# The first adaLN vector: scale and shift chunks side by side in one tile, accumulated by one operation of 512 columns

## The chip, the cores and the metric

The kernel runs on one core of one Trainium2 chip. The metric is the time of one execution on the device, in microseconds (us). A core has a matrix engine (TensorE, PE in the rows, with PEld for the loading of its weights), a vector engine (VectorE, DVE), a scalar engine (ScalarE, ACT), a general engine (GpSimd, POOL) and a sync engine (SyncE, SP, with SPq for its queue of transfers). Each engine executes its own instructions strictly in the order in which they stand; engines wait for each other by semaphores. SBUF is the on-chip memory of 128 partitions, PSUM the small memory into which TensorE writes its sums.

## What is computed

The kernel computes a decoder block: two kinds of attention side by side, then an MLP. Only its first step matters here. A condition vector `c` is multiplied by a wide matrix; the first 2048 of the resulting 6144 numbers are a shift and a scale for the normalised input `x`, and their result `h` feeds all projections.

```python
ada = (c @ w_ada + b_ada)[:, None, :]
shift1, scale1, gate1, shift2, scale2, gate2 = jnp.split(ada, 6, axis=-1)
h = rmsnorm(x, g_norm1) * (1.0 + scale1) + shift1
proj = h @ w_in
```

Here `c` has 1024 entries, `w_ada` is 1024 x 6144, `x` and `h` are 1024 x 1024 and `w_in` is 1024 x 5452, all in float32.

## The kernel before

The matrix products are done in three passes per block, with each operand split into a rounded high part and a low rest (`h_hi`, `h_lo`, `whi`, `wlo`; helper `mm3`), so every multiplication by `h` needs both parts.

The 1024 columns of `h` are worked on as eight chunks of 128, chunk 0 to 7. For a chunk, TensorE transposes two groups of four tiles of `x` into PSUM (tile `xT`, L265); ScalarE scales and shifts each group (`hf`, L272) and rounds it (`h_hi`, L273); GpSimd subtracts to get `h_lo` (L275). For the second groups of the last two chunks VectorE does all three (L268, L269, L275). The scale and shift of a chunk are columns of the small tile `ab`.

The scale and shift are made in five passes (list `KBS`, L229): pass 0 is chunk 0, pass 1 chunk 1, pass 2 chunks 2 and 3, pass 3 chunks 4 and 5, pass 4 chunks 6 and 7. For each pass `load_ada` (L206) fetches two blocks of `w_ada`, one for the scale (j = 1) and one for the shift (j = 0), into two of four buffers `wa`. In passes 0 and 1 the scale's sum over the 1024 rows is done by TensorE (L244). All the rest is done by VectorE: 8 operations in a row, each multiplying 128 or 256 columns of `wa` by an entry of `c` per partition and adding them to `acc` (L250 the first, L252 the other seven). The column sums of `acc` over the partitions are then taken by narrow TensorE products with a vector of ones (L179, shown in the rows as L75, `pv<-onesf,acc`), into the one PSUM bank `pv`, and VectorE adds the bias and writes `ab` (L180; for the scale also L183 and L184). Since there is only one bank `pv`, the column sums of one block can only start once L180 has read those of the block before.

As soon as chunks of `h` are there, TensorE multiplies them with the first weights: those of the indexer's key (in bank `S`, with `whi`), of its first two query heads (in bank `g`, with `whi`), and of its other two (with `qi_w`; first half of the sequence in bank `S`, second in bank `tr`). ScalarE and VectorE then unpack them (L360 to L372 into `KAi`, `QAi`, `QBi`, `misc`), and the index scores, the top-k search, attention and projections follow.

The order of the instructions on each engine isn't the order of the source: a list scheduler of the framework sets it from its own estimate of durations when the program is built, so a change of one operation can move many others. Block `with tc.high_priority()` (L235) puts this stage first.

Of the kernel before, what the change touches and what calls it, by code (L numbers as in the profile page):

```python
# [9 lines left out]
F32 = mybir.dt.float32  # L10
# [7 lines left out]
ALU = mybir.AluOpType  # L18
# [3 lines left out]
P = 128  # L22
D = 1024
S = 1024
KT = D // P
# [32 lines left out]
def block_kernel(ctx: ExitStack, tc: tile.TileContext, x, c, w_ada, b_ada, g_norm1, w_in, b_forget,  # L58
                 rel_bias, w_bf, w_bd, w_out, g_norm2, w_mlp1, w_mlp2, g_final, onehot, out):
    nc = tc.nc  # L60
# [3 lines left out]
    def pool(stack, name, bufs=1, **kw):  # L64
        if kw.get("space") != DRAM:
            kw.setdefault("reuse_waits", "tile")
        return stack.enter_context(tc.tile_pool(name=name, bufs=bufs, **kw))
# [6 lines left out]
    def mm(o, l, r, start, stop):  # L74
        nc.tensor.matmul(o, l, r, start=start, stop=stop)  # L75
# [15 lines left out]
    cT = vecT[:, 0:8]  # L91

    ab = cst.tile([P, 4, KT], F32, name="ab")
# [41 lines left out]
    def newton_rstd(pl, ss, n, tag, bufs=1):  # L135
        ms = pl.tile([P, n], F32, name="ms" + tag, tag="ms" + tag, bufs=bufs)
        nc.vector.tensor_scalar(ms, ss, 1.0 / D, EPS, op0=ALU.mult, op1=ALU.add)
        r = pl.tile([P, n], F32, name="rs" + tag, tag="rs" + tag, bufs=bufs)
        nc.scalar.activation(r, ms, AF.Sqrt)
        nc.vector.reciprocal(r, r)  # L140
        t = pl.tile([P, n], F32, name="nt" + tag, tag="nt" + tag, bufs=bufs)
        nc.vector.tensor_tensor(t, r, r, op=ALU.mult)
        nc.vector.tensor_tensor(t, t, ms, op=ALU.mult)
        nc.vector.tensor_scalar(t, t, -0.5, 1.5, op0=ALU.mult, op1=ALU.add)
        nc.vector.tensor_tensor(r, r, t, op=ALU.mult)
        return r
# [5 lines left out]
    ppv = pool(ps_stack, "ppv", 1, space=PSUM)  # L152
# [24 lines left out]
    def ada_cols(acc, j, k0, n, dst, ps, rows=P):  # L177
        for k in range(n):
            mm(ps[:, k:k + 1], acc[0:rows, k * P:(k + 1) * P], onesf[0:rows, 0:1], True, True)  # L179
        nc.vector.tensor_tensor(dst[:, k0:k0 + n], ps[:, 0:n], vecT[:, 24 + j * 8 + k0:24 + j * 8 + k0 + n], op=ALU.add)  # L180

    def norm_scale(dst, g0, n):
        nc.vector.tensor_scalar(dst, dst, 1.0, None, op0=ALU.add)  # L183
        nc.vector.tensor_tensor(dst, dst, vecT[:, g0:g0 + n], op=ALU.mult)  # L184
# [10 lines left out]
    wav = w_ada.rearrange("(k p) n -> p k n", p=P)  # L195
    with ExitStack() as st1:
        p1 = pool(st1, "p1")
        sqj = p1.tile([P, D], BF16, name="sqj")
        xn = [p1.tile([P, D], F32, name=f"xn{t}") for t in range(NTT)]
        ss = p1.tile([P, NTT], F32, name="ss")  # L200
        nc.scalar.activation(ss[:, 0:1], onesf[:, 0:1], AF.Sqrt)
        def load_x(ts_):
            for t in ts_:
                nc.sync.dma_start(xn[t], xr[t * P:(t + 1) * P, :])

        def load_ada(kt0, n):  # L206
            was = []
            for j in (1, 0):
                wt = p1.tile([P, KT, 256], F32, name="wa", tag="wa", bufs=4)[:, :, 0:n * P]
                nc.sync.dma_start(wt, wav[:, :, j * D + kt0 * P:j * D + (kt0 + n) * P])  # L210
                was.append((j, wt))
            return was

        def norm_x(g):
            for t in range(4 * g, 4 * g + 4):
                nc.scalar.activation(sqj, xn[t], AF.Square, accum_out=ss[:, t:t + 1])
            r = newton_rstd(p1, ss[:, 4 * g:4 * g + 4], 4, f"a{g}")
            for t in range(4 * g, 4 * g + 4):
                nc.vector.tensor_scalar(xn[t], xn[t], r[:, t - 4 * g:t - 4 * g + 1], None, op0=ALU.mult)

        load_x(range(4))
        nc.sync.dma_start(vecs[0:8, :], c.rearrange("o (k p) -> (o k) p", p=P))
        nc.sync.dma_start(vecs[8:16, :], g_norm1.rearrange("(k p) -> k p", p=P))
        nc.sync.dma_start(vecs[16:24, :], g_norm2.rearrange("(k p) -> k p", p=P))
        nc.sync.dma_start(vecs[24:72, :], b_ada.rearrange("(k p) -> k p", p=P))
        vps = ptr.tile([P, 512], F32, name="vps", tag="tr")
        nc.tensor.transpose(vps[:, 0:P], vecs, ident)
        nc.vector.tensor_copy(vecT, vps[:, 0:P])
        KBS = ((0, 1), (1, 1), (2, 2), (4, 2), (6, 2))  # L229
        was = load_ada(*KBS[0])  # L230
        load_x(range(4, 8))
        norm_x(0)
        nc.sync.dma_start(bfg[64:64 + NH, :], b_forget.rearrange("(h o) -> h o", o=1))
        first = [misc_weights(), split_w([(0, P, win[:, :, C_QI:C_QI + P])], nc.gpsimd)]
        with tc.high_priority():  # L235
            for kb, (kt0, n) in enumerate(KBS):
                if kb:
                    was = load_ada(kt0, n)
                for j, wt in was:
                    acc = p1.tile([P, 256], F32, name="acc", tag=f"acc{j}")[:, 0:n * P]  # L240
                    if j == 1 and kb < 2:
                        ps = ppv.tile([P, 512], F32, name="pv", tag="pv")
                        for k in range(KT):
                            mm(ps[0:1, 0:n * P], cT[:, k:k + 1], wt[:, k, :], k == 0, k == KT - 1)  # L244
                        nc.vector.tensor_copy(acc[0:1, :], ps[0:1, 0:n * P])
                        ada_cols(acc, j, kt0, n, ab[:, 1 - j, :], ppv.tile([P, 512], F32, name="pv", tag="pv"), 1)
                    else:
                        for k in range(KT):
                            if k == 0:
                                nc.vector.tensor_scalar(acc, wt[:, k, :], cT[:, 0:1], None, op0=ALU.mult)  # L250
                            else:
                                nc.vector.scalar_tensor_tensor(acc, wt[:, k, :], cT[:, k:k + 1], acc, op0=ALU.mult, op1=ALU.add)  # L252
                        ada_cols(acc, j, kt0, n, ab[:, 1 - j, :], ppv.tile([P, 512], F32, name="pv", tag="pv"))
                if kb == 0:
                    norm_x(1)
                if kb == len(KBS) - 1:
                    first.append(split_w([(0, P, win[:, :, C_QI + P:C_QI + 2 * P])], nc.gpsimd,
                                         dst=(qi_w[:, 0:1024], qi_w[:, 1024:2048])))
                norm_scale(ab[:, 0, kt0:kt0 + n], 8 + kt0, n)
                for k in range(kt0, kt0 + n):  # L260
                    for g in range(2):
                        gs = slice(g * 512, (g + 1) * 512)
                        ps = ptr.tile([P, 512], F32, name="xT", tag="tr")
                        for t in range(4):
                            nc.tensor.transpose(ps[:, t * P:(t + 1) * P], xn[4 * g + t][:, k * P:(k + 1) * P], ident)  # L265
                        hf = p1.tile([P, 512], F32, name="hf", tag="hf", bufs=4)
                        if kb == len(KBS) - 1 and g == 1:
                            nc.vector.tensor_scalar(hf, ps, ab[:, 0, k:k + 1], ab[:, 1, k:k + 1], op0=ALU.mult, op1=ALU.add)  # L268
                            nc.vector.tensor_copy(h_hi[:, k, gs], hf)  # L269
                            lo_eng = nc.vector  # L270
                        else:
                            nc.scalar.activation(hf, ps, AF.Identity, scale=ab[:, 0, k:k + 1], bias=ab[:, 1, k:k + 1])  # L272
                            nc.scalar.activation(h_hi[:, k, gs], hf, AF.Copy)  # L273
                            lo_eng = nc.gpsimd
                        lo_eng.tensor_tensor(h_lo[:, k, gs], hf, h_hi[:, k, gs].bitcast(F32), op=ALU.subtract)  # L275
# [499 lines left out]
    for half in range(2):  # L775
        sl = slice(half * 512, half * 512 + 512)
        for cp in range(4):
            hi, lo = split_w([(0, 256, wbv[1][:, :, cp * 256:cp * 256 + 256])], nc.gpsimd, 4)
            hv, lv = hi.rearrange("p (k c) -> p k c", k=4), lo.rearrange("p (k c) -> p k c", k=4)
            for c2 in range(2):  # L780
# [5 lines left out]
                ps = bank("q")  # L786
# [18 lines left out]
    with ExitStack() as st4:  # L805
# [6 lines left out]
        for ch in range(2):  # L812
# [3 lines left out]
            for t in range(NTT):  # L816
# [3 lines left out]
                ps = bank("q")  # L820
# [183 lines left out]
    with ExitStack() as st5:  # L1004
# [37 lines left out]
        def accumulate(ps, ut, tau, first, last, cs=slice(0, 512)):  # L1042
            tl = slice(tau * P, (tau + 1) * P)
            for i in range(2):
                for x, y in ((0, 2), (0, 3), (1, 2)):
                    mm(ps, ut[:, x, i, tl], ut[:, y, i, cs], first and i == 0 and (x, y) == (0, 2),
                       last and i == 1 and (x, y) == (1, 2))
# [65 lines left out]
        ps = run(step_24)  # L1113
# [8 lines left out]
        ps = run(step_35, lambda n: residual(1, 0, n))  # L1122
# [11 lines left out]
        ps = run(step_16, right_half)  # L1134
# [16 lines left out]
        ps = [bank("q")[:, 0:cs.stop - cs.start] for _, cs in cols]  # L1151
# [64 lines left out]
```

## Time and profile before

| | |
|---|---|
| median of 3 runs | 1632.06 us (1631.8 to 1632.16) |
| the profiled execution, its own time | 1634.09 us |
| its span, from first to last instruction | 1632.2 us |
| TensorE busy | 1565.2 us (96%) |
| VectorE busy | 1150.7 us (71%) |
| ScalarE busy | 947.4 us (58%) |
| GpSimd busy | 747.9 us (46%) |
| mean granted TensorE clock | 0.984 |

All times inside the program count from the start of the span. The durations come from this one execution. An instruction's duration may overlap the next one's by a few hundredths of a microsecond. The stage that the change touches lies in the first 90 us; the last chunk of `h` is complete at about 74 us.

### The profile page before, as it was taken

How to read it: one execution, taken by the hardware profiler on the slowest of the kernel's cores; microseconds unless marked ns; L12 is line 12 of the kernel's file. 1: busy time of each engine (PE TensorE's matmuls, PEld its weight loads, DVE VectorE, ACT ScalarE, POOL GpSimd, SP SyncE). 2: the span in 40 equal slices, each digit the busy share in tenths (PEclk: the TensorE clock that was granted, in tenths of full speed). 3: DMA queues.
4: the chain of work that ended last, by engine and by line, in shares of the span. 5: the costliest groups of instructions: out<-in, count | busy, mean ns of one | idle time of the engine just before them, and what ended most of it. 6: DMA issues, size and time to landing. Idle time of an engine off the chain costs nothing.

```text
span 1632.2 us, 22837 instructions
## 1 busy us (share of the span) xinstructions
PE 1565.2 (96%) x7585; PEld 1300.7 (80%) x7585; DVE 1150.7 (71%) x2230; ACT 947.4 (58%) x1689; POOL 747.9 (46%) x628
## 2 busy tenths in 40 slices
PE   4989999999989999999999998999999989999998
PEld 3777788887878888888888887888888868888887
DVE  6787777878897665567767547765555475758988
ACT  4454899898747777677663136554544343533433
POOL 3432222333335565656545301886666564343730
PEclk8999999999999999999999999999999989999999
DMA  9321222132124443544878456454444579655862
GB/s 301 81 47 51 61 79 57 44 80 49 53 63 147 116 138 100 155 139 142 304 242 292 126 187 215 141 167 152 151 142 143 181 287 344 231 207 193 268 222 103
DMA packets 223870, 253.01 MB, mean 155 GB/s; under 512 B 49137, under 2 KB 136257, under 8 KB 223753
## 3 DMA queue, kind: packets, MB, share of 16 engines
q1 hardware_dynamic: 215112, 233.73, 45.5%
q10 hardware_dynamic: 8640, 17.83, 2.9%
q8 instruction: 60, 0.98, 0.3%
q14 instruction: 58, 0.47, 0.1%
HBM read 186.48 MB, written 65.03 MB: 154 GB/s over the span
## 4 chain that ended last, share of the span: by engine, by line
PE 73%; DVE 10%; ACT 9%; DMA 4%; issue 2%; SPq 1%; POOL 1%; ACTq 0%; DVEq 0%; POOLq 0%
PE g L75 31%; PE S L75 24%; PE tr L75 8%; PE pv L75 7%; ACT eqt L495 4%; PE ptr L583 2%; ACT sp L567 1%; DVE acc L252 1%; DMA wap<-in_w_ada_dram 1%; ACT sp L570 1%; ACT ph L584 1%; DVE sp L563 1%; DVE pl L585 1%; DVE isc L434 1%; DMA gt<-G_d 1%
## 5 line engine op out<-in xcount | busy, mean ns | idle before, releaser
L75 PE MATMUL g<-h_hi,whi 128*128 128x512 f32 x656 | 264.5, 403 | 8.4 <-DVE KA L325 5.4
L75 PE MATMUL g<-h_hi,wlo 128*128 128x512 f32 x656 | 262.7, 400 | 0.0
L75 PE MATMUL g<-h_lo,whi 128*128 128x512 f32 x656 | 262.5, 400 | 0.0
L1039 DVE TENSOR_TENSOR ut<-rw,ut 128x1024 fp32r<-128x1024 f32 x112 | 182.0, 1670 | 66.3 <-ACT ut L1038 66.2
L123 POOL TENSOR_TENSOR wlo<-st,whi 128x1024 fp32r<-128x1024 f32 x60 | 148.6, 2477 | 110.7 <-ACT whi L122 103.0
L1038 ACT ACTIVATE ut<-rw 128x1024 fp32r<-128x1024 f32 x112 | 112.0, 1052 | 144.7 <-PE pv L75 66.6
L1053 POOL TENSOR_TENSOR rw<-rw 128x1024 f32<-128x1024 f32 x40 | 117.6, 2943 | 125.5 <-DMA rw<-in_w_mlp_dram 114.2
L75 PEld LDWEIGHTS g<-h_hi,whi 128*128 128x128 f32 x656 | 125.2, 191 | 34.1 <-issue 5.5
L75 PEld LDWEIGHTS g<-h_hi,wlo 128*128 128x128 f32 x656 | 124.7, 190 | 24.3
L75 PEld LDWEIGHTS g<-h_lo,whi 128*128 128x128 f32 x656 | 124.9, 190 | 22.5
L75 PE MATMUL S<-ut 128*128 128x512 f32 (+1 forms) x576 | 138.4, 385 | 0.0
L75 PEld LDWEIGHTS S<-ut 128*128 128x128 f32 x576 | 106.9, 191 | 21.2 <-DVE ut L1039 0.2
L585 DVE TENSOR_TENSOR pl<-ptr,ph 128x512 fp32r<-128x512 f32 (+1 forms) x160 | 99.8, 631 | 23.6 <-ACT ph L584 21.7
L567 ACT ACTIVATE sp<-sp,mn 128x128 f32<-128x128 f32 (+7 forms) x128 | 98.5, 771 | 25.5 <-DVE mn L563 25.2
L584 ACT ACTIVATE ph<-ptr 128x512 fp32r<-128x512 f32 (+1 forms) x160 | 86.4, 550 | 42.5 <-PE ptr L583 40.5
L495 ACT ACTIVATE eqt<-sel_all,nct 128x768 bf16<-128x768 int16 (+5 forms) x99 | 102.5, 1035 | 9.9 <-DVE nct L491 8.5
L570 ACT ACTIVATE sp<-sp,mn 128x128 f32<-128x128 f32 (+7 forms) x128 | 96.9, 770 | 18.6 <-DVE mn L569 18.1
L75 PE MATMUL g<-ut 128*128 128x512 f32 (+1 forms) x384 | 94.6, 381 | 6.0 <-ACT ut L1038 4.6
L583 PE MATMUL ptr<-ident,sp 128*128 128x128 f32 x576 | 89.8, 272 | 1.6 <-DVE nct L491 1.2
L122 ACT ACTIVATE whi<-st 128x1024 fp32r<-128x1024 f32 x51 | 53.8, 1055 | 62.3 <-DMA st<-in_w_mlp_dram 18.5
L75 PE MATMUL pv<-ph,V 128*128 128x256 f32 x320 | 85.2, 285 | 3.1 <-DVE yt L592 3.1
L75 PEld LDWEIGHTS g<-ut 128*128 128x128 f32 x384 | 70.0, 191 | 20.5 <-ACT ut L1038 5.0
(436 smaller groups left out, 3922.5 us busy)
## 6 DMA issues: line engine op xcount, KB each, us to landing
rw<-in_w_mlp_dram SPq DMA_DIRECT2D x72, 512.0 KB
rw<-U_d SPq DMA_DIRECT2D x56, 512.0 KB
wap<-in_w_ada_dram SPq DMA_DIRECT2D x64, 256.0 KB
st<-in_w_mlp_dram SPq DMA_DIRECT2D x32, 512.0 KB
st<-in_w_in_dram SPq DMA_DIRECT2D x26, 512.0 KB
U_d<-cc SPq DMA_DIRECT2D x48, 256.0 KB
st<-in_w_in_dram SPq DMA_DIRECT2D x33, 256.0 KB
G_d<-t SPq DMA_DIRECT2D x32, 256.0 KB
```

The source lines that it names most:

```text
L75: nc.tensor.matmul(o, l, r, start=start, stop=stop)
L122: nc.scalar.activation(hi, st, AF.Copy)
L123: (lo_eng or nc.vector).tensor_tensor(lo, st, hi.bitcast(F32), op=ALU.subtract)
L495: nc.scalar.activation(eqt[:, :(i + 1) * P], sel[i].bitcast(dt), AF.Sign, bias=nct[:, q], accum_out=cnt[:, q])
L567: nc.scalar.activation(sp[:, :W], sp[:, :W], AF.Exp, bias=mn[:, len(cs) - 1:len(cs)], scale=-1.0, accum_out=mn[:, 2:3])
L570: nc.scalar.activation(sp[:, :W], sp[:, :W], AF.Copy, scale=mn[:, 3:4])
L583: nc.tensor.transpose(tr[:, n * P:(n + 1) * P], pt[s][:, kb * P:(kb + 1) * P], ident)
L584: nc.scalar.activation(ph[:, z:], tr[:, z:], AF.Copy)
L585: nc.vector.tensor_tensor(pl[:, z:], tr[:, z:], ph[:, z:].bitcast(F32), op=ALU.subtract)
L1038: nc.scalar.activation(ut[:, n], t, AF.Copy)
L1039: nc.vector.tensor_tensor(ut[:, n + 1], t, ut[:, n].bitcast(F32), op=ALU.subtract)
L1053: nc.gpsimd.tensor_tensor(o, a, b, op=op)
```

## The change

The two blocks of a pass lie side by side in one buffer `wa` of twice the size (three such buffers instead of four single ones), still fetched by two transfers. In passes 2, 3 and 4 one operation of 512 columns accumulates scale and shift together, so a pass takes 8 operations on VectorE instead of 16. In passes 0 and 1 the work is as before. `acc` becomes one tile for both, with two buffers.

```diff
         def load_ada(kt0, n):
-            was = []
-            for j in (1, 0):
-                wt = p1.tile([P, KT, 256], F32, name="wa", tag="wa", bufs=4)[:, :, 0:n * P]
-                nc.sync.dma_start(wt, wav[:, :, j * D + kt0 * P:j * D + (kt0 + n) * P])
-                was.append((j, wt))
-            return was
+            wt = p1.tile([P, KT, 2, 256], F32, name="wa", tag="wa", bufs=3)[:, :, :, 0:n * P]
+            for v, j in enumerate((1, 0)):
+                nc.sync.dma_start(wt[:, :, v, :], wav[:, :, j * D + kt0 * P:j * D + (kt0 + n) * P])
+            return wt
...
-                for j, wt in was:
-                    acc = p1.tile([P, 256], F32, name="acc", tag=f"acc{j}")[:, 0:n * P]
-                    if j == 1 and kb < 2:
...
+                acc = p1.tile([P, 2, 256], F32, name="acc", tag="acc", bufs=2)[:, :, 0:n * P]
+                if kb < 2:
...
+                    accumulate(acc[:, 1, :], lambda k: was[:, k, 1, :])
+                else:
+                    accumulate(acc, lambda k: was[:, k])
+                for v, j in enumerate((1, 0)):
+                    ada_cols(acc[:, v, :], j, kt0, n, ab[:, 1 - j, :], ppv.tile([P, 512], F32, name="pv", tag="pv"),
+                             1 if j == 1 and kb < 2 else P)
```

The new function `accumulate` holds the loop of L248 to L252 unchanged. The scheduler then orders the program anew. On GpSimd, at the low parts of chunk 1 (the two `h_lo` after the first three rows) and the split of the weights `qi_w`, it stands before:

```order
L123 TENSOR_TENSOR wlo_184<-st_181,whi_183 128x1024
L275 TENSOR_TENSOR h_lo_119<-hf_247,h_hi_118 128x512
L123 TENSOR_TENSOR qi_w_110<-st_467,qi_w_110 128x1024
L275 TENSOR_TENSOR h_lo_119<-hf_288,h_hi_118 128x512
L275 TENSOR_TENSOR h_lo_119<-hf_297,h_hi_118 128x512
```

And now, in the same place:

```order
L123 TENSOR_TENSOR wlo_183<-st_180,whi_182 128x1024
L277 TENSOR_TENSOR h_lo_119<-hf_245,h_hi_118 128x512
L277 TENSOR_TENSOR h_lo_119<-hf_284,h_hi_118 128x512
L277 TENSOR_TENSOR h_lo_119<-hf_293,h_hi_118 128x512
L123 TENSOR_TENSOR qi_w_110<-st_433,qi_w_110 128x1024
```

The split of `qi_w` has gone behind the low parts of chunk 1. The transfer that it needs stands on SP's queue behind the two of pass 2 now, and ahead of them before.

On VectorE, at passes 3 and 4, it stands before (`acc_386` is the shift of pass 3, `acc_441` and `acc_454` scale and shift of pass 4, `pv_382` and `pv_395` the column sums of pass 3, `pv_450` and `pv_463` those of pass 4):

```order
L252 SCALAR_TENSOR_TENSOR acc_386<-wa_371,vecT_81,acc_386 128x256 x5
L180 TENSOR_TENSOR ab_83<-pv_382,vecT_81 128x2
L183 TENSOR_SCALAR ab_83<-ab_83 128x2
L184 TENSOR_TENSOR ab_83<-ab_83,vecT_81 128x2
L250 TENSOR_SCALAR acc_441<-wa_437,vecT_81 128x256
L252 SCALAR_TENSOR_TENSOR acc_441<-wa_437,vecT_81,acc_441 128x256
L180 TENSOR_TENSOR ab_83<-pv_395,vecT_81 128x2
L252 SCALAR_TENSOR_TENSOR acc_441<-wa_437,vecT_81,acc_441 128x256 x4
L250 TENSOR_SCALAR acc_454<-wa_439,vecT_81 128x256
```

And now (`acc_358` and `acc_416` hold both sums of passes 3 and 4, `pv_367` and `pv_371` are the column sums of pass 3, `pv_425` and `pv_429` those of pass 4):

```order
L242 SCALAR_TENSOR_TENSOR acc_358<-wa_355,vecT_81,acc_358 128x512 x7
L240 TENSOR_SCALAR acc_416<-wa_413,vecT_81 128x512
L242 SCALAR_TENSOR_TENSOR acc_416<-wa_413,vecT_81,acc_416 128x512 x6
L180 TENSOR_TENSOR ab_83<-pv_367,vecT_81 128x2
L242 SCALAR_TENSOR_TENSOR acc_416<-wa_413,vecT_81,acc_416 128x512
L183 TENSOR_SCALAR ab_83<-ab_83 128x2
L184 TENSOR_TENSOR ab_83<-ab_83,vecT_81 128x2
L180 TENSOR_TENSOR ab_83<-pv_371,vecT_81 128x2
L180 TENSOR_TENSOR ab_83<-pv_425,vecT_81 128x2
L183 TENSOR_SCALAR ab_83<-ab_83 128x2
L184 TENSOR_TENSOR ab_83<-ab_83,vecT_81 128x2
L180 TENSOR_TENSOR ab_83<-pv_429,vecT_81 128x2
```

The scale of pass 3 is now written behind seven of the eight operations of pass 4, and the shift of pass 3 behind the eighth; before, both were written when pass 4 had hardly begun.

On TensorE, ahead of the transposes of chunk 5, it stands before (`S_656` is the product with `qi_w`):

```order
L75 MATMUL g_623<-h_hi_118,wlo_184 128x512
L75 MATMUL S_656<-h_lo_119,qi_w_110 128x512
L75 MATMUL S_656<-h_hi_118,qi_w_110 128x512
L265 MATMUL xT_419<-ident_66,xn0_124 128x128
L265 MATMUL xT_419<-ident_66,xn1_125 128x128
```

And now:

```order
L75 MATMUL g_589<-h_hi_118,wlo_183 128x512
L75 MATMUL pv_371<-onesf_71,acc_358 128x1 x2
L75 MATMUL pv_425<-onesf_71,acc_416 128x1 x2
L75 MATMUL pv_429<-onesf_71,acc_416 128x1 x2
L267 MATMUL xT_395<-ident_66,xn0_124 128x128
L267 MATMUL xT_395<-ident_66,xn1_125 128x128
```

The column sums of pass 4, which before stood 23 and 43 rows behind the first of these transposes, have moved ahead of the transposes of chunk 5. Behind this stage the order differs in many small places up to about the middle of the program (on TensorE up to row 2692 of 5123), and not after that.

## Rows read from the trace of the kernel before

**Rows 1.** Page, part 1: engine, busy us (share of the span), x instructions.

```profile
PE 1565.2 (96%) x7585; PEld 1300.7 (80%) x7585; DVE 1150.7 (71%) x2230; ACT 947.4 (58%) x1689; POOL 747.9 (46%) x628
```

**Rows 2.** Timeline, ScalarE: start us, us, engine, line, operation, out<-in, xcount, [idle before <-releaser].

```profile
28.21 1.06 ACT L122 ACTIVATE qi_w<-st 128x1024 fp32r<-128x1024 f32 x1 [0.21 <-DMA st<-in_w_in_dram]
...
46.23 1.45 ACT L272 ACTIVATE hf<-xT,ab 128x512 f32<-128x512 f32 x2 [8.80 <-DVE ab L180]
...
56.84 1.45 ACT L272 ACTIVATE hf<-xT,ab 128x512 f32<-128x512 f32 x2 [5.75 <-DVE ab L180]
```

**Rows 3.** Timeline, GpSimd, 0 to 100 us.

```profile
31.16 2.38 POOL L123 TENSOR_TENSOR qi_w<-st,qi_w 128x1024 fp32r<-128x1024 f32 x1
36.99 2.82 POOL L275 TENSOR_TENSOR h_lo<-hf,h_hi 128x512 fp32r<-128x512 f32 x2 [3.45 <-ACT h_hi L273]
48.27 5.92 POOL L275 TENSOR_TENSOR h_lo<-hf,h_hi 128x512 fp32r<-128x512 f32 x4 [8.47 <-ACT h_hi L273]
...
70.08 3.08 POOL L275 TENSOR_TENSOR h_lo<-hf,h_hi 128x512 fp32r<-128x512 f32 x2 [5.64 <-ACT h_hi L273]
```

**Rows 4.** Timeline, VectorE, 0 to 100 us.

```profile
31.38 2.31 DVE L252 SCALAR_TENSOR_TENSOR acc<-wa,vecT,acc 128x128 f32<-128x128 f32 x1
...
33.72 0.35 DVE L252 SCALAR_TENSOR_TENSOR acc<-wa,vecT,acc 128x128 f32<-128x128 f32 x1
...
34.83 0.34 DVE L250 TENSOR_SCALAR acc<-wa,vecT 128x256 f32<-128x256 f32 x1
...
43.49 2.58 DVE L252 SCALAR_TENSOR_TENSOR acc<-wa,vecT,acc 128x256 f32<-128x256 f32 x6
...
46.31 8.17 DVE L252 SCALAR_TENSOR_TENSOR acc<-wa,vecT,acc 128x256 f32<-128x256 f32 x10
...
56.66 2.04 DVE L252 SCALAR_TENSOR_TENSOR acc<-wa,vecT,acc 128x256 f32<-128x256 f32 x4
...
68.30 0.16 DVE L180 TENSOR_TENSOR ab<-pv,vecT 128x2 f32<-128x2 f32 x1 [0.91 <-PE pv L75]
...
72.04 1.66 DVE L275 TENSOR_TENSOR h_lo<-hf,h_hi 128x512 fp32r<-128x512 f32 x1
```

**Rows 5.** Line L1164 of VectorE, durations ns min/median/max.

```profile
L1164 DVE SCALAR_TENSOR_TENSOR C<-C,rsc,gfb x8: 742/747/753, 1607.1 to 1613.4; 128x512 f32<-128x512 f32 x8
```

**Rows 6.** Transfers from 26 to 35 us.

```profile
DMA packets 3330, 3.06 MB, mean 340 GB/s; under 512 B 48, under 2 KB 3329, under 8 KB 3329
```

**Rows 7.** Timeline, TensorE, 54 to 64 us.

```profile
58.11 1.04 PE L265 MATMUL xT<-ident,xn 128*128 128x128 f32 x8
...
63.37 0.60 PE L75 MATMUL pv<-onesf,acc 128*128 128x1 f32 x4 [1.22 <-DVE acc L252]
```

**Rows 8.** Timeline, TensorE, 82 to 87 us.

```profile
82.45 0.39 PE L75 MATMUL tr<-h_hi,qi_w 128*128 128x512 f32 x1
...
83.87 0.41 PE L75 MATMUL S<-KAi,QAi 128*128 128x384 f32 x1 [0.39 <-DVE QAi L362]
85.91 0.44 PE L75 MATMUL S<-KAi,QBi 128*128 128x384 f32 x1 [1.63 <-DVE QBi L363]
```

**Rows 9.** Windows of 4 us: busy us of each engine, clock, DMA share, GB/s.

```profile
core 0: us, PE busy (x) PEld busy (x) DVE busy (x) ACT busy (x) POOL busy (x), PEclk, DMA share, GB/s
...
44.00:48.00 4.00, 2.13 (x12) 1.64 (x11) 3.96 (x12) 1.77 (x3) 0.00 (x0) 0.83 1.16 235
48.00:52.00 4.00, 4.00 (x21) 3.51 (x20) 3.89 (x5) 3.09 (x6) 3.73 (x3) 0.74 1.05 351
84.00:88.00 4.00, 2.26 (x8) 1.50 (x9) 3.77 (x11) 1.86 (x5) 0.00 (x0) 0.95 0.54 150
88.00:92.00 4.00, 4.00 (x12) 3.18 (x12) 3.75 (x11) 3.27 (x4) 0.00 (x0) 0.62 0.00 0
```

**Rows 10.** Who TensorE waited for, 84 to 128 us: us, times, longest.

```profile
PE S L75 <- ACT rl L429: 2.6, 2, 2.2
...
PE g L75 <- DVE KA L325: 1.6, 1, 1.6
```

More of the change, by code (lines that the diff above doesn't have):

```diff
@@ L238, in block_kernel, with accumulate @@
                     was = load_ada(kt0, n)
-                for j, wt in was:
-                    acc = p1.tile([P, 256], F32, name="acc", tag=f"acc{j}")[:, 0:n * P]
-                    if j == 1 and kb < 2:
[L242 to L253, printed above, removed]
+                def accumulate(acc, src):
+                    for k in range(KT):
+                        if k == 0:
+                            nc.vector.tensor_scalar(acc, src(k), cT[:, 0:1], None, op0=ALU.mult)
+                        else:
+                            nc.vector.scalar_tensor_tensor(acc, src(k), cT[:, k:k + 1], acc, op0=ALU.mult, op1=ALU.add)
+                acc = p1.tile([P, 2, 256], F32, name="acc", tag="acc", bufs=2)[:, :, 0:n * P]
+                if kb < 2:
+                    ps = ppv.tile([P, 512], F32, name="pv", tag="pv")
+                    for k in range(KT):
+                        mm(ps[0:1, 0:n * P], cT[:, k:k + 1], was[:, k, 0, :], k == 0, k == KT - 1)
+                    nc.vector.tensor_copy(acc[0:1, 0, :], ps[0:1, 0:n * P])
+                    accumulate(acc[:, 1, :], lambda k: was[:, k, 1, :])
+                else:
+                    accumulate(acc, lambda k: was[:, k])
+                for v, j in enumerate((1, 0)):
+                    ada_cols(acc[:, v, :], j, kt0, n, ab[:, 1 - j, :], ppv.tile([P, 512], F32, name="pv", tag="pv"),
+                             1 if j == 1 and kb < 2 else P)
                 if kb == 0:
```

## The prediction

> **What bounds the kernel now.** I read the page's first part first: TensorE is busy 96% of the span [rows 1], so a gain anywhere else counts only where TensorE stands idle or at its slow clock. The chain of waits for the first 120 us then shows where that is: up to about 50 us it runs mostly over VectorE's accumulations of the adaLN vector, and from there over TensorE. The timelines of the single engines are the main view. On ScalarE the reader is to see that chunks 2 and 4 of `h` start at 46.23 and 56.84 us, after long waits [rows 2]. On TensorE, that the products with `h` still wait 1.22 us at 63.37 and then run until 82.45 [rows 7, 8]. Behind that point it waits 0.39 and 1.63 us for VectorE, which only now unpacks what all these products left [rows 8]. The windows show the third cost, the clock: after a stretch in which TensorE was busy 2.13 us of 4, the granted clock is 0.83 and then 0.74, and after one of 2.26 us it is 0.95 and then 0.62 [rows 9]. A mean of 0.74 is a part at 1.2 GHz and a part at 2.4. Work done is in proportion to the clock, so the loss is (0.17 + 0.26) x 4 = 1.72 us in the one place and (0.05 + 0.38) x 4 = 1.72 us in the other.
>
> **The cost of the accumulation.** A 256-column operation takes a step of 0.52 us when it waits for the one before it on the same `acc`: four of them take 2.04 us, (2.04 - 0.48) / 3, with 0.48 the duration of one. Where operations of two sums alternate, as the scheduler had them for half of the time, the step is only (2.58 - 0.48) / 5 = 0.42 [rows 4]. A free 512-column operation of the same kind takes 0.747 us [rows 5]. The seven of a pass now all hang on each other, so I count 0.78 for each and 0.50 for the first one (a one-input operation whose 256 columns took 0.34 [rows 4], with more columns and a step). An old pair alternating costs 0.84, the new one 0.78: most of what the fewer operations save was already hidden by alternating. On its own the change would shorten VectorE's 24 operations by 1 to 4 us, depending on how many pairs alternated.
>
> **The cost of GpSimd beside it.** While GpSimd subtracts, VectorE's two-input operations stretch: one of 128 columns took 2.31 us beside the split of `qi_w` (31.16 to 33.54) and 0.35 without it, so 1.96 are lost; ten of 256 columns took 8.17 beside four `h_lo`, (8.17 - 0.48 - 9 x 0.42) / 4 = 0.98 lost for each [rows 3, 4]. A 512-column subtraction on VectorE beside GpSimd took 1.66 us [rows 3, 4], and I take 1.66 for a new operation that meets an `h_lo`. Nearest bounds: 1.39, if only the old loss less the hidden step is added to the new width, and 2.2, a free one plus a whole `h_lo` of 2.82 / 2 = 1.41 [rows 3]. The Trainium skill, "Trainium Architecture — The Big Picture", section "What this means for kernel authors", says that the two engines' shared port is an exclusive lock, not a division of bandwidth. By that rule the whole `h_lo` would be lost and 2.2 would hold; the 0.98 above is less than the 1.41, so I stay with the row. By the rule the sum below would come out 3.2 us later (six meetings of 0.54), at +1.5 us.
>
> **The walk through the new order**, in the times of before. Up to 31.4 us the engines' orders agree.
> - The split of `qi_w` has gone behind chunk 1's low parts, so the last accumulations of pass 1 don't meet it: -1.96 us, and pass 2 starts at 34.83 - 1.96 = 32.9 us instead of 34.83 [rows 4]. The wide operation needs both blocks of pass 2. Their 2 x 1.05 MB at 340 GB/s take 6.2 us [rows 6]; they follow the transfer before last, which I put at 0.52 MB or 1.5 us ahead of the last one, landed by 28.2 [rows 2]: 26.7 + 6.2 = 32.9. So this edit costs nothing only just, and up to 1 us if the landing is late. The weights `qi_w` land at about 34.4 now; GpSimd takes them after chunk 1, which hides it.
> - Pass 2: 0.50 + 4 x 0.78 free, two beside chunk 1's `h_lo` at 1.66, one beside `qi_w` at 0.75 + 1.96: 9.65, so 42.5. Then two column sums one after the other through the one bank, each 0.60 on TensorE [rows 7] and 0.16 on VectorE [rows 4]: 44.0. Chunk 2 starts on ScalarE at 44.1, 2.1 us before the old 46.23.
> - Pass 3 starts at 44.0. GpSimd's `h_lo` begin 48.27 - 46.23 = 2.04 after ScalarE [rows 2, 3], at 46.1. Three operations run free to 46.3, four meet an `h_lo`: 46.3 + 4 x 1.66 = 53.0.
> - Here the new order costs. The scale of pass 3 is written behind seven operations of pass 4: 53.0 + 0.5 + 6 x 0.78 + 0.16 = 58.3; the shift behind the eighth and two small ones: 59.5. Chunk 4 starts on ScalarE at 59.6, 2.8 us after the old 56.84 [rows 2]. No `h_lo` falls into this stretch, since none is ready.
> - TensorE, in order, stands at the column sums of pass 4: 59.5 + 0.60 + 0.16 + 0.60 = 60.9 before it may transpose chunk 5, against 58.11 [rows 7]. Behind that come the same 84 products and 24 transposes in both orders. They took 82.45 - 58.11 = 24.3 us, less the wait of 1.22 and two pairs of column sums of 0.60 that no longer stand there: 21.9. All of pass 4 is known by then, so nothing more waits for it: 60.9 + 21.9 = 82.8, +0.35 us.
> - TensorE has run out of work at about 55 (pass 3 ends at 53.0, and eight products are left), so it is idle for most of 55 to 60.9. After each of the two such stretches of before a slow one followed; I count one, +1.7.
> - Behind 82.45: the first half of the indexer's key is now complete some 40 products before the end of this block, where before both halves ended together. VectorE unpacks it meanwhile, so the waits of 0.39 and 1.63 [rows 8] and the slow stretch after them, 1.72 [rows 9], should go: -3.7. Bounds: 0, if VectorE is late again for another reason, and -3.7 together with 2 of the 4.2 us of later waits for `rl` and `KA` [rows 10], if VectorE's lead lasts.
>
> Sum: +0.35 + 1.7 - 3.7 = -1.7 us. The profiled execution took 1634.09 us for a span of 1632.2; its time lies 2.0 above the median of 1632.06, and a difference carries over: 1632.06 - 1.7 = 1630.4 us.
>
> Not priced are the many small changes of order up to the middle of the program. The rows show single waits of TensorE of 1.6 and 2.2 us [rows 10] that such an order makes or removes, so I allow about two of either sign with nothing at the centre, +-4 us.
>
> **The rivals.** What a measurement of this kernel can tell from no change is about 0.2%, 3.3 us.
> - Faster: the clock doesn't fall around 60 us, and VectorE's lead lasts past the waits for `rl` and `KA`: 0.35 - 3.7 - 2 = -5.4, 1626.7 us. For it: VectorE is the engine that TensorE waits for there. Against it: 5 idle microseconds are more than those after which the clock fell before. Chance 0.26.
> - No effect: wide operations gain nothing, since their old pairs alternated, and what the order moves cancels: 1632 us. It is the rival by which the change doesn't do what it is to do. For it: 0.84 against 0.78. Against it: the wait of 1.96 for `qi_w` goes in any case. Chance 0.14.
> - Slower: the column sums of pass 4 in front of chunk 5 hold TensorE up for longer. If a wide operation costs 2.2 beside GpSimd, six meetings move this point to 64.1; TensorE then has some 8 us without work, two slow stretches instead of one: 64.1 + 21.9 + 3.4 = 89.4 instead of 82.45, +7.0, and only the 2.0 of waits are won back behind it: +5.0, 1637.0 us. It decides from about 62 us on. For it: all four sums now hang in a row behind 15 operations of VectorE. Against it: four `h_lo` of chunks 4 and 5 no longer meet any accumulation. Chance 0.22.
> - My forecast has 0.38, all of it within 3.3 us of before.
>
> **How the numbers follow.** Faster by over 0.2%: 0.26. Within 0.2%: 0.38 + 0.14 = 0.52. Slower: 0.22. The likeliest case with its unpriced order gives 1626.4 to 1634.4. A range that leaves out no more than a tenth on each side reaches over the middle of both outer rivals: 1625 to 1637 us.
>
> **What would show it.** Right: `qi_w` on GpSimd behind two `h_lo`; chunk 2 on ScalarE at about 44 and chunk 4 at about 59.6 us; TensorE with an idle stretch of 3 to 5 us before the transposes of chunk 5 and a clock below 1 after it; the block of products ending between 82 and 85 us; no wait for `QBi` behind it. Wrong: a wide operation far from 0.78 us free and 1.66 beside GpSimd, chunk 4 not later than before, or a gain or loss that lies behind 100 us.

## The result: 15 us slower, and nearly all of it behind the changed stage

| | median, us | range (5 runs) | span of the profiled execution |
|---|---|---|---|
| before | 1632.16 | 1631.8 to 1634.05 | 1632.2 |
| after | 1647.31 | 1646.84 to 1649.63 | 1644.8 |

The ratio is 1.0095, 95% interval 1.0080 to 1.0109; that is 15.5 us, 13.1 to 17.8. The forecast of 1630.4 us had the wrong sign, and its range to 1637 us missed the time. Part 1 of the page of after answers to [rows 1]:

```profile
PE 1575.0 (96%) x7585; PEld 1309.4 (80%) x7585; DVE 1140.5 (69%) x2206; ACT 948.8 (58%) x1689; POOL 740.5 (45%) x628
```

VectorE has 24 instructions and 10.2 us less. TensorE has the same 7585 instructions and is busy 9.8 us longer: more of them ran at the slow clock, and the mean granted clock of the span is 0.975 where it was 0.984. Its idle time grew as well, by 2.8 us (span less busy: 69.8, before 67.0).

**The stage went nearly as forecast.** VectorE, in the timeline of after (columns as in [rows 4]):

```profile
33.32 9.30 DVE L242 SCALAR_TENSOR_TENSOR acc<-wa,vecT,acc 128x512 f32<-128x512 f32 x7
...
44.34 9.13 DVE L242 SCALAR_TENSOR_TENSOR acc<-wa,vecT,acc 128x512 f32<-128x512 f32 x7
...
53.90 4.69 DVE L242 SCALAR_TENSOR_TENSOR acc<-wa,vecT,acc 128x512 f32<-128x512 f32 x6
58.51 0.15 DVE L180 TENSOR_TENSOR ab<-pv,vecT 128x2 f32<-128x2 f32 x1
```

Six operations with nothing beside them took 4.69 us, 0.78 each as forecast. The scale of pass 3 is written by 58.7 us (58.3). Chunks 2 and 4 start on ScalarE at 44.5 and 59.8 us (44.1 and 59.6), where [rows 2] had 46.23 and 56.84:

```profile
44.52 1.45 ACT L274 ACTIVATE hf<-xT,ab 128x512 f32<-128x512 f32 x2 [8.18 <-DVE ab L180]
...
59.82 0.78 ACT L274 ACTIVATE hf<-xT,ab 128x512 f32<-128x512 f32 x1 [10.25 <-DVE ab L180]
```

The last product of the block starts on TensorE at 84.46 us; the walk's 82.8 with the slow stretch of 1.7 makes 84.5. One sign in it did not come: TensorE still had products until 57.2 us, so it stood idle for 2.2 us in three pieces, the first of them shown here, and not for 3 to 5.

```profile
58.71 0.61 PE L75 MATMUL pv<-onesf,acc 128*128 128x1 f32 x4 [1.47 <-DVE ab L180]
```

The larger error lies behind the block. First the windows of after, then whom TensorE waited for in 83 to 125 us (us, times, longest), against [rows 8 to 10]:

```profile
56.00:60.00 4.00, 2.08 (x12) 1.44 (x11) 3.58 (x9) 0.18 (x1) 0.00 (x0) 1.00 0.00 0
60.00:64.00 4.00, 3.75 (x19) 3.47 (x19) 0.65 (x4) 3.82 (x7) 2.14 (x2) 0.62 0.01 2
64.00:68.00 4.00, 4.00 (x23) 3.29 (x22) 0.68 (x1) 2.37 (x5) 2.82 (x3) 0.95 0.00 0
84.00:88.00 4.00, 2.89 (x16) 1.64 (x14) 3.84 (x7) 0.00 (x0) 1.19 (x1) 1.00 0.86 239
88.00:92.00 4.00, 4.00 (x13) 3.16 (x13) 3.75 (x10) 1.93 (x4) 0.00 (x0) 0.57 0.07 20
```

```profile
PE S L75 <- ACT rl L431: 2.5, 2, 2.2
PE wps L384 <- DVE misc L373: 0.8, 1, 0.8
PE g L75 <- DVE QBi L363: 0.3, 1, 0.3
```

The waits of 0.39 and 1.63 us became 0.77 and 0.34: 0.9 us won instead of 2.0. The slow stretch at 88 us is still there, (1 - 0.57) x 4 = 1.72 us. Of the 3.7 us counted as won, 0.9 came. Why `misc` came late stands in the timelines of GpSimd and VectorE:

```profile
80.39 4.80 POOL L123 TENSOR_TENSOR wlo<-st,whi 128x1024 fp32r<-128x1024 f32 x2 [8.21 <-ACT whi L122]
```

```profile
80.48 2.45 DVE L364 CAST QAi<-QAi 64x256 fp32r<-64x256 f32 x1
82.86 2.68 DVE L365 CAST QBi<-QBi 64x256 fp32r<-64x256 f32 x2
85.57 0.76 DVE L373 TENSOR_SCALAR misc<-S,bfg 64x512 f32<-64x512 f32 x1
```

Three casts, which take 0.29 us each when GpSimd is idle, took 5.06 us beside GpSimd's two splits of weights, and `misc` stood behind them.

**Where the 15 us are.** TensorE executes the same 7585 products in every kernel here, so the start of the n-th, less the start of the first, can be set against that of before; the difference is called the offset. Where the order differs the n-th need not be the same product. The first product starts 9.5 us into the span of before, so a time in this table is 9.5 us less than in the timelines. One profile each, in us:

| product | before, us after the first | after | new stage, old order | old stage, new order | spread | spread, loads later | local moves |
|---|---|---|---|---|---|---|---|
| 300 | 82.6 | +1.2 | +0.1 | -3.0 | 0.0 | -1.1 | -1.1 |
| 500 | 131.3 | +3.5 | +1.5 | 0.0 | 0.0 | -1.4 | -1.0 |
| 800 | 196.2 | +6.6 | +1.4 | +2.8 | 0.0 | -1.4 | -1.0 |
| 1900 | 408.4 | +5.2 | +2.3 | +1.4 | +0.1 | -1.3 | -0.2 |
| 2200 | 474.4 | +14.7 | +3.0 | +10.7 | -9.9 | -11.3 | -4.2 |
| 2300 | 493.7 | +13.6 | +3.0 | +9.7 | -9.4 | -10.7 | -1.6 |
| 2400 | 511.6 | +13.7 | +3.0 | +9.8 | +10.0 | -1.4 | -1.6 |
| 3000 | 620.8 | +14.9 | +3.0 | +11.0 | +9.9 | +4.2 | -1.6 |
| 7500 | 1601.0 | +12.7 | +0.7 | +7.5 | +8.4 | +5.9 | -1.9 |

Product 300 starts at 92 us of the span. There, behind the stage and the unpacking, after is 1.2 us late. Up to product 500 it loses 2.3 us more, up to product 800 another 3.1, wins 1.4 back, loses 8.4 between products 1900 and 2300 (418 to 503 us of the span), and little after that. The two earlier losses, in windows of before and then of after:

```profile
100.00:120.00 20.00, 18.43 (x87) 14.97 (x86) 16.15 (x22) 11.48 (x23) 9.11 (x7) 1.00 0.25 43
180.00:200.00 20.00, 18.61 (x102) 15.62 (x101) 17.02 (x47) 18.15 (x38) 6.42 (x9) 1.00 0.16 35
```

```profile
100.00:120.00 20.00, 17.61 (x79) 14.18 (x78) 16.97 (x23) 10.79 (x22) 8.08 (x6) 0.91 0.26 43
180.00:200.00 20.00, 16.23 (x84) 13.93 (x83) 17.18 (x56) 19.55 (x38) 6.01 (x8) 0.85 0.09 19
```

In each, after has a slow stretch that before does not have, besides more waiting. In the first the slow stretch comes to (1 - 0.91) x 20 = 1.8 us, and the waits of 92 to 142 us to 5.2 instead of 4.4. In the stretch from 470 us of the span the windows of before and of after read:

```profile
470.00:480.00 10.00, 7.09 (x23) 5.38 (x24) 9.94 (x15) 5.31 (x10) 7.27 (x5) 0.84 0.03 9
480.00:490.00 10.00, 10.00 (x53) 8.51 (x53) 9.87 (x19) 3.56 (x9) 1.52 (x2) 0.99 0.29 61
```

```profile
470.00:480.00 10.00, 6.85 (x23) 4.34 (x22) 10.00 (x23) 4.06 (x9) 5.27 (x2) 0.70 0.01 3
480.00:490.00 10.00, 4.31 (x21) 3.08 (x21) 9.97 (x18) 7.52 (x13) 4.75 (x6) 0.67 0.54 128
```

VectorE is full in both (third busy column): this is where it writes out the top-k selection (`select_tile`) beside the attention. Before, TensorE has other work meanwhile, 53 products in the second window; in the new order the independent projections (`g`) stood earlier, 21 products are left, and it waits 5.7 us, then runs slowly. Of the products into `g` the two windows of before hold 20 and 32, those of after 3 and none. The timelines show the longest wait on TensorE, and what VectorE does in it:

```profile
489.78 0.90 PE L585 MATMUL ptr<-ident,sp 128*128 128x128 f32 x3 [4.04 <-DVE pl L587]
```

```profile
485.55 0.14 DVE L530 TENSOR_TENSOR need<-need,cnt 128x1 f32<-128x1 f32 x1
485.62 1.27 DVE L532 SCALAR_TENSOR_TENSOR bjunk<-isc,Thi,bjunk 128x1024 bf16<-128x1024 int16 x1
486.81 0.14 DVE L571 RECIPROCAL mn<-mn 128x1 f32<-128x1 f32 x1
486.88 2.26 DVE L534 TENSOR_TENSOR_SCAN sel_all<-eqt 128x1024 uint16<-128x1024 bf16 x1
489.07 0.65 DVE L587 TENSOR_TENSOR pl<-ptr,ph 128x512 fp32r<-128x512 f32 x1
```

Three rows of the selection stand ahead of `pl`, for which TensorE stands still. Nothing needs the finished selection yet: VectorE masks the first scores with it at 543.6 us.

### The profile page after: what moved, and what is told of

It is laid out like the page before. It is cut to its first block, busy times and chain, and to the rows that moved or that the text cites. A ratio compares the mean times of both kernels' runs of the same rounds, so it can differ in the third digit from the quotient of the medians.

```text
span 1644.8 us, 22795 instructions
## 1 busy us (share of the span) xinstructions
PE 1575.0 (96%) x7585; PEld 1309.4 (80%) x7585; DVE 1140.5 (69%) x2206; ACT 948.8 (58%) x1689; POOL 740.5 (45%) x628
## 4 chain that ended last, share of the span: by engine, by line
PE 81%; DVE 9%; DMA 4%; issue 2%; ACT 2%; POOL 1%; SPq 0%; ACTq 0%; DVEq 0%; POOLq 0%
PE g L75 37%; PE S L75 24%; PE tr L75 8%; PE pv L75 8%; PE ptr L585 3%; DVE acc L242 2%; DMA wap<-in_w_ada_dram 1%; DMA wa<-in_w_ada_dram 1%; DVE pl L587 1%; DMA gt<-G_d 1%; ACT eqt L497 1%; DMA t<-G_d 1%; DVE sp L565 1%; DVE bjunk L500 1%; DVE sel_all L534 0%
## 5 line engine op out<-in xcount | busy, mean ns | idle before, releaser
L1055 POOL TENSOR_TENSOR rw<-rw 128x1024 f32<-128x1024 f32 x40 | 113.7, 2845 | 127.4 <-DMA rw<-in_w_mlp_dram 110.1
L120 POOL CAST whi<-st 128x1024 fp32r<-128x1024 f32 x23 | 24.5, 1065 | 140.1 <-PE g L75 106.5
L75 PE MATMUL pv<-pl,V 128*128 128x256 f32 x320 | 83.9, 289 | 2.8 <-DVE pl L587 2.8
```

The lines of the kernel that those rows point to most:

```text
L1055: nc.gpsimd.tensor_tensor(o, a, b, op=op)
```

## Experiments

Theory A: the loss comes from the order that the scheduler gave to the rest of the program. Rival B: it comes from the changed stage itself. Ratios are to the kernel before on the same chip, whose median was 1632.9 to 1633.6 us.

| kernel | median, us | ratio to before | 95% interval |
|---|---|---|---|
| new stage, old order | 1635.20 | 1.0009 | 1.0000 to 1.0019 |
| old stage, new order | 1644.70 | 1.0069 | 1.0053 to 1.0085 |
| tile alone | 1636.69 | 1.0033 | 1.0018 to 1.0048 |
| moved rows | 1644.24 | 1.0067 | 1.0052 to 1.0082 |
| wide in pass 2 only | 1654.23 | 1.0128 | 1.0108 to 1.0148 |
| wide in passes 3, 4 only | 1650.83 | 1.0107 | 1.0092 to 1.0122 |
| repaired new order | 1648.71 | 1.0091 | 1.0076 to 1.0106 |
| repaired, loads later | 1642.37 | 1.0054 | 1.0037 to 1.0071 |
| before, spread | 1642.33 | 1.0050 | 1.0033 to 1.0067 |
| before, spread, loads later | 1638.21 | 1.0036 | 1.0023 to 1.0049 |
| before, loads later | 1639.26 | 1.0041 | 1.0025 to 1.0057 |
| before, local moves | 1630.00 | 0.9976 | 0.9965 to 0.9986 |

**Stage and order exchanged.** Behind the stage the two kernels' source is the same, instruction for instruction, so the order of one can be imposed on the other: each engine's instructions are chained in the order of a table.

```diff
+    tail = len(nc.cur_bb.bb.instructions)      # behind the stage
     def gemm_h(hi, lo, half, pl=None):
...
+    for a, c in zip(row, row[1:]):             # row: one engine's order
+        tc.add_manual_dep(ins[c], ins[a].name, <order only>)
```

> The changed first stage (wide accumulations, their own order), but behind the stage every engine's rows stand in the order of the kernel before. Theory A (the loss sits in the order that the scheduler gives the rest of the program): the offset against before stays at about +1 to +2 us, which is what the trace shows at the stage's end (+1.2 at 83 us), so 1632 to 1635 us. Rival B (the loss comes from the stage itself, its later chunk 4 and its lumped column sums, and the waits further on only pass it on): 1644 to 1648 us, since the stage is the changed one.

> The first stage of the kernel before (256-column accumulations), but behind the stage every engine's rows stand in the order of the changed kernel. Theory A: the loss is here without the change, 1644 to 1648 us, with TensorE's long wait for the low part of the probabilities at about 486 us. Rival B: 1631 to 1634 us.

The changed stage in front of the old order costs 0.09%, 1.5 us; the old stage in front of the new order costs 0.69%, 11.3 us. The sum, 12.8, differs from the whole 15.5 by less than their intervals: the order's part alone lies between 8.7 and 13.9. The trace says the same: from product 300 to product 3000 the new order loses 14.0 us behind the old stage and 13.7 behind the new one. The window and the timeline of TensorE show the same hole without the change:

```profile
480.00:490.00 10.00, 6.25 (x21) 4.80 (x21) 9.87 (x17) 6.65 (x11) 5.34 (x4) 0.50 0.72 212
```

```profile
486.73 0.90 PE L585 MATMUL ptr<-ident,sp 128*128 128x128 f32 x3 [3.75 <-DVE pl L587]
```

For this change theory A holds and B falls. One limit: inside the stage the scheduler was free, and with the old order behind it put chunk 2 at 49.1 us and chunk 4 at 60.5, not at 44.5 and 59.8. The 1.5 us are therefore the price of the wide operations in a stage ordered otherwise.

**Parts of the change.**

The tile alone is the kernel before with `load_ada` as in the change:

```diff
-                for j, wt in was:
+                for v, j in enumerate((1, 0)):
+                    wt = was[:, :, v, :]
```

The other two are the changed kernel, here the one that is wide in pass 2 only (the other has `kb > 2`):

```diff
-                    accumulate(acc, lambda k: was[:, k])
+                    if kb == 2:
+                        accumulate(acc, lambda k: was[:, k])
+                    else:
+                        accumulate(acc[:, 0, :], lambda k: was[:, k, 0, :])
+                        accumulate(acc[:, 1, :], lambda k: was[:, k, 1, :])
```

> The weight blocks side by side in one tile of 3 buffers as in the change, but accumulated in two sums of 256 columns as before; the scheduler orders freely and leaves nearly all rows behind the stage where they stood. Theory A: no reordering, so 1631 to 1635 us. If the tile itself (both blocks freed together, 3 buffers of 2.1 MB in place of 4 of 1.05) costs the time, 1640 us or more, with later transfers of the weights at 25 to 45 us.

> The changed kernel, but only pass 2 is accumulated by one operation of 512 columns; passes 3 and 4 run as two sums of 256 columns in the same tile. The scheduler orders freely and puts some 3000 of TensorE's 5100 rows elsewhere than in either kernel. Theory A: what the order behind the stage costs has nothing to do with how many operations are wide, so this comes out anywhere from 1628 to 1648 us, and more than 3 us of its distance from before arise behind 100 us. Rival B (the loss is caused by the wide operations): a third of the change's loss, 1636 to 1638 us, all of it made by 90 us.

> The changed kernel, but only passes 3 and 4 are accumulated by operations of 512 columns; pass 2 runs as two sums of 256 columns in the same tile. Theory A: again an order of its own behind the stage and a time anywhere from 1628 to 1648 us, made behind 100 us. Rival B: two thirds of the change's loss, 1641 to 1643 us, made by 90 us.

With the tile alone TensorE's order as built differs from that of before in 328 places, none behind the 539th product, against 2383 places with the change; and its offset does not grow behind product 300: +5.6 us there, +5.7 at 500, +5.8 at 1900, +1.5 at 7500. So the tile costs time up to product 300, with chunk 4 at 58.4 us instead of 56.84; with the wide operations as well it is +1.2. My expectation of 1631 to 1635 missed by 2 us for that reason. Half the change costs more than the whole: rival B's proportion (1636 to 1638, 1641 to 1643) is refuted. Theory A's numbers fail too: 1654 and 1651 us lie above its 1648, and about half of it (+10.8 and +6.7 us) exists already at product 300, where waits for `QBi` and `QAi` of 1.7 to 3.4 us had come in; that these too come from the order no run shows. Behind product 300 the offsets grow from 10.8 to 20.9 and from 6.7 to 16.6. These two are the only other kernels in which the scheduler put most rows elsewhere; with the change that is three of three slower than before, by 15 to 21 us.

**Rows moved in the new order.** On VectorE, at 485 us (and likewise one scan at 471 us; two rows on ScalarE):

```diff
-need<-need,cnt
-bjunk<-isc,Thi,bjunk 128x1024
-sel_all<-eqt 128x1024
 pl<-ptr,ph 128x512
...
 pl<-ptr,ph 128x512
+need<-need,cnt
+bjunk<-isc,Thi,bjunk 128x1024
+sel_all<-eqt 128x1024
```

> The changed kernel in its own order, with 4 rows of VectorE and 2 of ScalarE moved: at 471.6 us the scan of the selection goes behind the two subtractions that make the low part of the probabilities, at 485.6 to 489.1 us three rows of the selection go behind the two such subtractions that follow them, and on ScalarE the copy of the high part goes ahead of an exponential and a copy of KA. Theory A: TensorE's waits of 1.75 and 4.04 us fall to under 1 us each and the slow clock after them goes in part, 3 to 6.5 us less: 1641 to 1644 us. If VectorE, which is busy all through 440 to 495 us, only passes the wait on to the next operation: 1646 to 1648 us. Rival B says nothing of this place and expects no more than the waits' 4 us, at 1643 us or above.

The wait of 4.04 us is down to 0.59, the one of 1.75 is gone, and the kernel is at +10.9 us instead of +15.5, 1644.2 for an expected 1641 to 1644 (the intervals of the two ratios just touch). By the trace 2 us of it stay won (11.6 for 13.6 at product 2300); the rest went into a wait that was 0.77 us long, at a row that now stands behind the moved scan (timeline of TensorE):

```profile
479.24 0.66 PE L75 MATMUL S<-KA,QA 128*128 128x512 f32 x1 [3.96 <-DVE mn L567]
...
488.34 0.90 PE L587 MATMUL ptr<-ident,sp 128*128 128x128 f32 x3 [0.59 <-DVE pl L589]
```

That is rival C: where VectorE is full, a row that is put back falls in front of the next one that TensorE needs.

**The selection spread out.** 54 rows of VectorE spread evenly up to the first masked attention, in both orders:

```diff
-[the 54 rows of select_tile among 59 (before: 53) others, 429 to 496 us]
+[the same rows among 82 (before: 78) others, one for every 1.5]
```

> The changed kernel in its own order, with rows moved at the two places where its trace loses time. VectorE: the 54 rows that write out the selection (429 to 496 us) are spread evenly over all its rows up to the first masked attention. At 191 us: ScalarE makes two copies of the high part of the probabilities ahead of two copies of QA and an exponential, and VectorE their low parts ahead of counts of the search. Theory A, by which the loss is these rows standing ahead of what TensorE waits for: the offset against before no longer grows from 3.0 to 6.6 us at 196 us, and hardly at 450 to 495 us; 3 us and 6 to 8 us less than the changed kernel: 1636 to 1639 us. Rival C (VectorE is simply full there, whatever its order, and the wait turns up at the next row as it did where 4 rows were moved): 1642 to 1645 us.

> The kernel before in its own order, only the 54 rows of VectorE that write out the selection spread evenly over its rows up to the first masked attention. TensorE waits 8.4 us in 440 to 500 us of the kernel before (10 - 8.48, 9.11, 8.51, 7.09 us of each 10). If VectorE's selection rows in front of the attention's are what it waits for, 4 to 8 us of that go: 1625 to 1629 us, faster than both kernels. Rival C: 1631 to 1634 us.

Both came out the opposite way: 1648.7 and 1642.3 us. The table says why. Up to product 2300 the spread does what it should: -9.4 us, TensorE hardly waits. Then it stops for 11.5 us (in the kernel before; 10.8 in the new order), which the table shows at product 2400. The timelines of TensorE and ScalarE and the waits of SyncE's queue (us, times, longest) around it, in the kernel before:

```profile
522.79 0.58 PE L75 MATMUL pv<-ph,V 128*128 128x256 f32 x1 [11.51 <-DVE yt L594]
```

```profile
521.29 0.60 ACT L611 ACTIVATE t<-g 128x512 f32<-128x512 f32 x1 [16.19 <-DMA G_d<-t]
```

```profile
SPq L651 <- DVE bjunk L532: 34.3, 1, 34.3
```

SyncE's queue stood 34 us in front of loads that overwrite `isc`, the selection's input, whose last read had moved to 509.8 us. Behind these loads stood the store `G_d<-t`; ScalarE's next row waited for the buffer of that store, the copy `yt` stood behind this row, and TensorE waited for `yt`. At 191 us the two copies moved ahead in the new order gained nothing either: TensorE then waited 4.71 us for `yt`, the next row behind the same counts, instead of 3.22 for `ph`.

**The loads moved too.**

```diff
-[SyncE: 8 x isc<-Y_d, ready at about 490 us]
...
 toep<-T_d 128x256
+[SyncE: 8 x isc<-Y_d, at about 556 us]
```

> The kernel before with the 54 selection rows of VectorE spread evenly, and on SyncE's queue the eight loads that overwrite the selection's input (isc) moved some 40 rows later, to about 550 us; they are used at about 620 us. Theory D (the spread did take away TensorE's waits at 440 to 500 us, 9.9 us by the trace, and lost them again because these loads stood in the queue waiting 34 us for the last read of isc, with the stores and weights that ScalarE needs behind them): the stop of 11.5 us at 511 us is gone, and the 9 us stay won: 1622 to 1627 us. Rival C (VectorE is full, and the work put off stops TensorE later in any case): 1631 to 1642 us.

> The changed kernel in its own order, repaired as before at 191 us and in 429 to 530 us, with the same eight loads moved later on SyncE's queue. Theory D: the stop of 10.8 us at 510 us is gone, and what the trace of the repair showed at 494 us, +1.1 us against before, stays to the end: 1632 to 1636 us, so that nearly all of the change's 15 us is undone by moving rows behind the stage. Rival B (the loss sits in the stage): 1645 us or more. Rival C: 1640 to 1648 us.

> The control: the kernel before with only the eight loads moved later on SyncE's queue, and the selection where it was. Theory D: in the kernel before the queue stands for 7.6 us in front of these loads and is free at 490 us, when nothing waits for what is behind, so 1630 to 1634 us. If the loads alone cost the kernel before its waits at 440 to 490 us: 1624 to 1628 us.

Theory D holds for the stop: 11.5 us become a wait of 1.95, and 10 of the 19 us lost between products 2300 and 2400 come back. It fails for the time: 1638.2 and 1642.4 us. In the new order the loads gave 0.37% back; in the kernel before the two intervals overlap. The 9 us won by product 2300 are spent by product 2400 in the same way as before, since the last tile of the selection now meets a full VectorE there and the granted clock is 0.71 and 0.50 in 505 to 515 us. The control shows a second price: with the loads at 556 us the kernel before loses 0.41%. Its trace loses 2.9 us between products 2400 and 2800, with a new wait of 2.7 us for a zeroing by GpSimd; the rest of the control's loss its one profile doesn't show.

**Five rows moved in the kernel before**, each behind or ahead of the row that TensorE waits for (two of the four places):

```diff
-need   bjunk<-isc,Thi,bjunk   V<-vtr,V   sel_all<-eqt   KA<-g,KA     (443 us)
+need   KA<-g,KA   bjunk<-isc,Thi,bjunk   V<-vtr,V   sel_all<-eqt
-eqt<-isc,Thi,eqt   need   yt<-pv,yt   bjunk   KA<-g,KA     (472 us)
+yt<-pv,yt   KA<-g,KA   eqt<-isc,Thi,eqt   need   bjunk
```

> The kernel before with five rows of VectorE moved past each other in 440 to 480 us and nothing else: a half of KA ahead of two rows and a scan of the selection (443.2 us), one selection row behind the minimum of a score tile and a low part (454.8), one behind another minimum (468.2), and yt and a half of KA ahead of three selection rows (472.1). Its trace shows TensorE waiting there for just these rows: 1.52 us for KA, 0.89 and 1.48 for the minima, 1.57 for yt, 1.34 for KA, 6.8 us in all, and a slow clock at 475 to 480 us worth 1.65. Theory A (what a selection row costs is decided by who stands right behind it): 4 to 7 us less and no new stop further on, since the selection ends less than 3 us later: 1625 to 1629 us. Rival C (VectorE is full in this stretch, so the wait goes to the next row behind): 1631 to 1634 us.

1630.0 us, 0.24% faster than before (0.14 to 0.35%): 3.9 us faster than before and faster than both kernels, a little less than expected. The windows of before for 470 to 480 us stand above (7.09 us busy at clock 0.84); with the moves:

```profile
440.00:450.00 10.00, 9.46 (x47) 7.36 (x45) 9.90 (x21) 5.14 (x12) 4.08 (x4) 1.00 0.00 0
...
470.00:480.00 10.00, 9.09 (x45) 7.12 (x45) 9.90 (x16) 4.74 (x10) 5.18 (x5) 1.00 0.03 8
480.00:490.00 10.00, 8.62 (x43) 6.48 (x42) 9.87 (x19) 3.11 (x9) 4.17 (x4) 1.00 0.30 61
```

4.2 us are won by product 2200 and 2.6 of them lost again by 2300: TensorE is busy 8.62 us in 480 to 490, where before it was busy all 10. So A and C share the truth: the order decides what is lost, but in this stretch, where VectorE is full, part of each gain moves on. What no run tested is the other half of the reading, the missing products: none put the products into `g` alone back to where the old order has them.

## Why the prediction was wrong

- **The step that failed** is the term for the new order behind the stage: "the many small changes of order up to the middle of the program", for which the prediction allowed "about two of either sign with nothing at the centre, +-4 us". The reorder measured by itself cost 11.3 us, 0.53 to 0.85% of the time. I took single waits of 1.6 and 2.2 us for its unit. In the trace the unit is larger: a stretch of 60 us in which VectorE is full, where the question is whether TensorE has unrelated products to do. In 470 to 490 us it had hardly any left, the waits added up, and the slow clock followed. That stretch stood in the trace of before at 430 to 500 us and I did not read it. Nor was the centre at nothing: the two other kernels with most rows elsewhere were slower still.
- **The second step** is the gain behind the block, -3.7. It is 0.9: VectorE had half the key in time, but the new order put three casts beside GpSimd's splits, `misc` came behind them, and the slow stretch stayed. This is 2.8 us of error, and -1.7 + 2.8 = +1.1 is what the trace shows at product 300 (+1.2). The old stage in front of the new order has the same two waits, 0.77 and 0.34 us, but no slow stretch after them (granted clock 1.00 in 84 to 92 us), and stands at -3.0 there. So the waits belong to the order; why the slow stretch came in one case and not in the other these runs do not show.
- **Accumulation:** right. 0.78 free. Beside GpSimd pass 3 gives (9.13 - 3 x 0.78) / 4 = 1.70 for 1.66. The loss of 0.92 per meeting is again less than one `h_lo`, 6.36 / 4 = 1.59 in GpSimd's timeline:

```profile
38.45 2.84 POOL L123 TENSOR_TENSOR qi_w<-st,qi_w 128x1024 fp32r<-128x1024 f32 x1
46.56 6.36 POOL L277 TENSOR_TENSOR h_lo<-hf,h_hi 128x512 fp32r<-128x512 f32 x4 [5.28 <-ACT h_hi L275]
```

  The Trainium skill ("Trainium Architecture — The Big Picture", "What this means for kernel authors") calls the port that the two engines share an exclusive lock, by which all of it would be lost. For these operations the trace does not agree, as the prediction held; for the three casts above, which lost 4.2 of the 4.8 us of GpSimd's splits, it nearly does. One price did not hold for every operation of VectorE. The prediction's lower bound of 1.39 does not follow from its words: the old loss of 0.98 less the hidden step of 0.10, added to 0.78, is 1.66.
- **Split of `qi_w` behind chunk 1, chunks 2 and 4, and the slow stretch after 60 us, (0.38 + 0.05) x 4 = 1.72 us:** right, to 0.4 us. Two readings in this part were off without moving the sum. The walk counts seven of the eight operations of pass 3; the first, 0.49 us, ran between the two column sums in front of it. And the idle stretch was 2.2 us, since TensorE had more than the eight products that the walk left it; that one slow stretch came all the same is in part luck.
- **The rivals:** "slower" came, by another mechanism than I wrote. The column sums held TensorE to 61 us, not beyond the 62 from which that rival was to decide.
- The prediction named its own refutation: "a gain or loss that lies behind 100 us".

What stays open: of the four kernels whose rows are the same up to product 500, three have the slow stretch at 115 to 120 us (after, repaired with loads later, moved rows: granted clock 0.66, 0.70 and 0.76) and lose 2.3, 2.0 and 2.0 us from product 300 on; the repaired order has a clock of 1.00 there and loses 0.3. So this loss comes with the slow stretch, and why one profile lacks it these runs do not show. And whether an order exists that keeps the 9 us won before product 2300 was not found here.

## What to carry to other kernels

Where a scheduler orders the whole program, a change in one stage is two changes: price the stage, then impose the old order behind it and measure the rest apart. For the second, look in the trace of before for the stretches where a supporting engine is full and see what the bounding engine has to do in them; the largest loss here lay where its independent work had been taken away. When a producer's rows are put off, follow who waits to overwrite what they read: here a load at the head of an in-order queue stopped everything behind it.

## What the runs showed of the hardware that was not expected

- A load that waited for its buffer held SyncE's queue for 34.3 us, and a row of 0.60 us on ScalarE waited 16.2 us for a store that stood behind this load.
- Beside GpSimd's subtractions VectorE lost 0.92 us of each `h_lo` of 1.59 with a wide accumulation, but 4.2 us of two splits' 4.8 with three small casts.
- TensorE's slow clock is paid in busy time: with the same 7585 instructions it was busy 9.8 us longer. A product of 512 columns started every 0.23 us at full clock (495.20, 495.43, 495.65 us in after) and every 0.43 us at half (491.95, 492.38, 492.80 us).
